# Entering a gated recurrence: one summed view of squares, and gate sums and weights put off

## The chip, the cores and the metric

The kernel runs on one core of a Trainium2 chip. The metric is the device time of one execution in microseconds. TensorE (PE in the profile, PEld for its weight loads) multiplies matrices into PSUM banks; VectorE (DVE), ScalarE (ACT) and GpSimd (POOL) work on elements; SyncE's queue (SPq) issues the DMAs of this kernel. Each engine takes its instructions in the order in which the finished program lists them, so an instruction that waits holds up everything behind it in its own queue.

## The reference

A trunk of two layers over 1024 tokens of width 1024. Each layer adds a token mixer and then a SwiGLU channel mixer to the residual; before each stands an RMS norm, modulated by shift and scale from a conditioning vector. Layer 0 mixes with a forgetting attention of 16 heads, layer 1 with gated linear attention (GLA) of 4 heads. What the change touches is the entry to layer 1's mixer, cut here to its core:

```python
h = modulate(rms_norm(x, norm1_g[i]), sh1, sc1)
q, k, v, r, a_lr = split(h @ w_in)
log_alpha = log_sigmoid(a_lr @ w_a2 + b_a) / GLA_TAU
b = cumsum(log_alpha, per chunk)          # the gate sums
q_in, k_in = q * exp(b), k * exp(-b)
o_intra = where(tril, q_in @ k_in.T, 0) @ v
k_dec = k * exp(b_last - b);  kv = k_dec.T @ v
S = exp(b_last) * S + kv;     o = o_intra + q_in @ S_prev
o = rms_norm(o) * g_o * silu(r)
```

Everything is float32. The kernel keeps that precision by splitting each matmul operand into a high part (rounded to the matmul's number format) and a low part (the rest) and adding three products: high by high, high by low, low by high.

## The kernel before, in words

Activations lie with the features on the partitions: eight tiles of 128 features by 1024 tokens, handled in two halves of 512 tokens. The mixer's normalized input is `h1`, eight pairs `h1[k].hi` and `.lo` (in the profile `h1h`, `h1l`).

**The entry.** The last block of layer 0's channel mixer finishes `x` tile by tile (L1156). `SumSq` squares each finished tile on ScalarE (L663) and adds squares in a tree (L670) on VectorE and GpSimd. For the second half it leaves four views unadded: the sum of squares 0 to 3, that of 4 and 5, square 6, and square 7. They are handed to `norm_mixer` (L1639), which for the second half keeps them in `half1`, and then issues `late_low`: two low parts of the first half's `h1` (L637) that were put off.

After that TensorE computes values and the gate's low-rank input for head 0: `gva(tp, ...)` makes 48 products of 272 columns for two token tiles, in three groups (high by high, high by low, low by high) of 2 x 8. `in_turn` lists 96 of them for `tp` 0 and 1, all of which need the first half of `h1` alone, and puts small matmuls of the second half's norm between them, one behind each product as the list `rms_later(..., each=13)` says: `sums(i, t)` (L597) sums view `i` of token tile `t` over the partitions with a vector of ones; `root` takes the mean (DVE, L606) and its power -1/2 (POOL, L607); after 13 more products `row(t)` (L613) spreads the result over the partitions; then `norm_half` makes the second half of `h1` from it on VectorE, ScalarE and GpSimd. Behind these 96 follow the keys of half 0, values of `tp` 2 (with the first gate product `gate_z` between), values of `tp` 3, queries of half 0, keys of half 1 (L2004, L1708).

**Gate sums.** `gate_z` (L1760) gives the gate's logits; `gate_sum` makes the logarithm of the sigmoid (ACT, L1770 and L1771; DVE, L1772) and its running sum per block of 128 tokens (DVE scan, L1775). For the next head this is done ahead by the generator `gate_ahead(h + 1)`: its first step does `gate_z`, its second `gate_sum` and a DMA that stores the result in `gsum_d` (L1785); `gate_back` (L1791) reads it back later. The two slots of the ring `kdr` serve both the sums made ahead (`b16a`, `t2a`) and the pair `kd` (`kdh`, `kdl`), the transposed decayed keys that `kd_trans` (L1820) makes, so `kdh` waits for the store.

**Queries and recurrence.** `head_front` multiplies query products by the gates' exponentials (L1863, tile `gy`, from the PSUM tile `gqp`) and splits them (L164, L165: `gq00`, `gq01`). `head_back` does the products within chunks (`at`, `ahl`, `go`) and the states (`kv`, `S_t`); `weave` alternates it with `r_proj`, the output gate's products (`gr`). Then the next head's values follow (`gv`).

**Weights.** `feed` is one list of weight loads in the order of use: for head 0 keys, queries and two output-gate weights, then for head 1 two value weights (`wv_0`, `wv_4`), keys and so on. A load is one DMA on SP, two casts on ScalarE (L207, high part) and four subtractions on GpSimd (L210, low part). `feed.fill()` loads until `feed.depth` weights lie ready.

**What sets the order.** The program is traced through a tile framework that simulates a timeline to put each engine's instructions in order before anything runs. `tc.issue_after(ins)` (and `tied`, which takes several) adds an order without a semaphore: what the block traces on the engine of `ins` stands behind `ins` in that engine's queue. `last_of("D")` is the instruction traced last on VectorE, "A" ScalarE, "P" TensorE, "G" GpSimd. Beside all this, `ada1` feeds in pieces of the next modulation (DMA L405, ACT L423, POOL L425).

Of the kernel before, what the change touches and what calls it, by code (L numbers as in the profile page):

```python
# [16 lines left out]
P = 128  # L17
S = 1024
D = 1024
# [35 lines left out]
def trunk(ctx, tc, x, c, ada_w, ada_b, norm1_g, norm2_g, ffn_w_in, ffn_w_out,  # L55
# [534 lines left out]
    def rms_later(ss, nm, psr, then, each=0):  # L590
# [26 lines left out]
                then(at["rb"])  # L617

        if each:
            one = [f for i in range(len(ss)) for t in range(4) for f in (None, lambda i=i, t=t: sums(i, t))]  # L620
            return one + [root] + [None] * each + [lambda t=t: row(t) for t in range(4)]
        return ([None] * 2 + [lambda t=t: sums(0, t) for t in range(4)] + [None] * 2
                + [lambda t=t: rest(t) for t in range(4)] + [root] + [None] * 6
# [1014 lines left out]

    def norm_mixer(hf, ss, tmp):  # L1639
        if hf:  # L1640
            half1.extend((ss, tmp))
            with tc.issue_after(last_of("D")):
                for low in late_low:
                    low()
            return
        hs1.extend(new_h("h1"))
        rb = rms_rows(ss, "100", Ring(psp, ["b3", "b4"]))
        gates = [(SPM, sp_ins[-1]), (RBM, last_ins())]
        norm_half(xs, hs1, 1, 0, rb, tmp)
        return gates  # L1650
# [53 lines left out]
    def gva(tp, w, ring, at):  # L1704

        ps = [ring([P, VA], F32, f"gva{tp}{i}") for i in range(2)]
        ks = [(w[k // 3], k % 3) for k in range(8)]
        mm = lambda i, a_, b_, s0=False, s1=False: lambda: nc.tensor.matmul(ps[i], a_, b_, start=s0, stop=s1)  # L1708
        hs = lambda part, k, i: getattr(h1[k], part)[:, psl(2 * tp + i)]
        products = []  # L1710
        for i in range(2):
            products += [mm(i, hs("hi", k, i), w_.hi[:, j, :], s0=k == 0) for k, (w_, j) in enumerate(ks)]
        for i in range(2):
            products += [mm(i, hs("hi", k, i), w_.lo[:, j, :]) for k, (w_, j) in enumerate(ks)]
        for i in range(2):
            products += [mm(i, hs("lo", k, i), w_.hi[:, j, :], s1=k == 7) for k, (w_, j) in enumerate(ks)]

        def evac():
            v = vr([P, 2, 2, 256], FR, f"gvt0{tp}")
            for i in range(2):  # L1720
                nc.vector.tensor_copy(at(2 * tp + i), ps[i][:, 256:VA])
            for i in range(2):
                split(v[:, 0, i], v[:, 1, i], ps[i][:, 0:256])
            return v
        return products, evac
# [112 lines left out]
    def head_front(h, b16, t2, ei, nmid, kin=None, wq=None, q0=None):  # L1838
# [14 lines left out]
        for hf in range(2):  # L1853
# [9 lines left out]
                nc.vector.scalar_tensor_tensor(y, ps, QS, f[:, cs], op0=ALU.mult, op1=ALU.mult)  # L1863
                split(t.hi[:, cs], t.lo[:, cs], y)
            if not h:
                next(ahead, None)
            elif not hf:
                kd = kd_tiles(h)
                kd_trans(h, kd, t2, 0)
        if not h:  # L1870
            kd = kd_tiles(h)
            kd_trans(h, kd, t2, 0)
        return kin, qt, kd
# [15 lines left out]
    def head_back(h, kin, qt, kd, t2, dec, vt, gs, need):  # L1889
# [44 lines left out]
        for g in range(2):  # L1934
            ahl = intra(g)
            yield 1.3
            if g == 0:
                kd_trans(h, kd, t2, 1)
                sp[1] = state(0)
                yield 0.79  # L1940
                if h < 3:
                    gnext.append(gate_back(h + 1))
# [66 lines left out]
    def second(rb):  # L2009
# [3 lines left out]

    p0, evac0 = gva(0, wv, pj, atok)
    p1, evac1 = gva(1, wv, pj, atok)
    in_turn(p0 + p1, rms_later(half1[0], "101", Ring(psp, ["b3", "b4"]),
                               second, 13))
    vt = [evac0(), evac1()]
    kin = key_tiles(0)
# [8 lines left out]
    in_turn(listed(k0, wk, 0), [None] * 10 + turns, last_of("P"))  # L2028
    ends()
    p2, evac2 = gva(2, wv, pj, atok)  # L2030
    in_turn(p2, [None] * 24 + [lambda: gate_z(0, (0,), bt)], last_of("P"))
    to0 = sm.tile([P, 4, NB], F32, tag="dec", name="dec0"), Tr([P, S], F32, "ei0")
    vt.append(evac2())
    gate_sum(0, bt, (0,))
# [1 line left out]
    key_evac(kin, k0, 0, *bt, to0[1], to0[0][:, 2])  # L2036
    ada1(5.1)
    p3, evac3 = gva(3, wv, pj, atok)
    in_turn(p3, [], last_of("P"))
    vt.append(evac3())  # L2040
    feed.depth = 1
    wq = feed.next()
# [6 lines left out]
    in_turn(listed(k1, wk, 1), [None] * 6 + [lambda: gate_z(0, (1,), bt)], last_of("P"))  # L2049
    k1_last = last_of("P")  # L2050
    gate_sum(0, bt, (1,))
    with tied(last_of("A")):
        feed.fill()
    b16, t2, ei, dec = gate_exps(0, bt, (1,), to0)
    key_evac(kin, k1, 1, b16, t2, ei, dec[1])
    for _ in range(3):
# [111 lines left out]
```

## Time and profile before

| what | value |
|---|---|
| runs | 2408.58, 2413.9, 2415.01 us; median 2413.9 |
| profiled execution | 2415.17 us, span 2413.3 us |
| mean granted TensorE clock | 0.994 |
| TensorE busy | 2370.4 us, 98% of the span |
| entrance of the recurrence | about 1312 to 1405 us of the span |
| HBM traffic | 269.25 MB read, 90.24 MB written |

A row of the timeline has the start in us from the span's start, the time in us, the engine, the line of the kernel, the operation, written tile and read tiles, the shape, and `xN` where N instructions are merged; in brackets stands how long the engine sat idle before it and what released it. A row of stretches has the limits, the length, the busy time and number of instructions of each engine, the granted clock (1.00 is full speed) and the share and rate of DMA.

### The profile page before, as it was taken

What the parts mean: (1) busy time and instruction counts of PE and PEld (TensorE: products, weight loads), DVE (VectorE), ACT (ScalarE), POOL (GpSimd) and SP (SyncE); (2) the same over time, 40 slices, a digit from 0 to 9 for tenths busy, and PEclk for the clock granted to TensorE, in tenths of its full rate; (3) what the DMA queues carried; (4) which work ended last, traced back from release to release, by engine and by line L of the source; (5) the groups of instructions that cost most, each with busy time, mean ns of one, the idle gap of its engine ahead of it and who ended that gap; (6) DMA issues with size and microseconds to landing.
All of it is one profiled execution on the core that took longest, in us unless ns stands there. A gap on an engine that the chain in (4) does not pass through costs nothing.

```text
span 2413.3 us, 36035 instructions
## 1 busy us (share of the span) xinstructions
PE 2370.4 (98%) x12318; PEld 2017.3 (84%) x12318; DVE 1675.1 (69%) x2794; ACT 1186.9 (49%) x2285; POOL 1206.7 (50%) x1074
## 2 busy tenths in 40 slices
PE   7999999999999999999999999999999999999998
PEld 6888888878888888888888888898888888888888
DVE  6577677676687877876687645446586767666787
ACT  4665556666544444445324756564344333345325
POOL 3343344433337878853364546573345656653362
PEclk9999999999999999999999999999999999999999
DMA  9233333123335555457665334445325434347664
GB/s 273 70 107 114 97 111 108 62 94 117 127 100 179 184 167 178 158 182 259 227 205 164 83 110 123 127 129 177 113 84 174 165 133 150 134 172 260 225 208 147
DMA packets 329407, 361.88 MB, mean 150 GB/s; under 512 B 24508, under 2 KB 253016, under 8 KB 329224
## 3 DMA queue, kind: packets, MB, share of 16 engines
q1 hardware_dynamic: 329032, 359.57, 46.2%
q8 instruction: 97, 1.59, 0.3%
q14 instruction: 86, 0.70, 0.1%
q10 hardware_dynamic: 192, 0.02, 0.0%
HBM read 269.25 MB, written 90.24 MB: 149 GB/s over the span
## 4 chain that ended last, share of the span: by engine, by line
PE 88%; ACT 3%; DVE 3%; DMA 2%; issue 1%; SPq 1%; POOL 1%; DVEq 0%; POOLq 0%; ACTq 0%
PE p_b L263 16%; PE p_b L262 16%; PE p_b L261 16%; PE o_b L1061 2%; PE t_b L1047 2%; PE qk_b L261 2%; PE qk_b L262 2%; PE qk_b L263 2%; PE s_b L1016 1%; PE s_b L1017 1%; PE gr_b L262 1%; PE gr_b L263 1%; PE vps_b L261 1%; PE gr_b L261 1%; PE vps_b L262 1%
## 5 line engine op out<-in xcount | busy, mean ns | idle before, releaser
L165 DVE TENSOR_TENSOR o_s<-xv_s,o_s 128x512 fp32r<-128x512 f32 (+1 forms) x376 | 338.0, 902 | 76.3 <-ACT o_s L164 75.7
L164 ACT CAST o_s<-xv_s 128x512 fp32r<-128x512 f32 (+1 forms) x376 | 218.0, 587 | 330.9 <-PE p_b L263 267.5
L1027 POOL TENSOR_SCALAR lp_s<-lp_s,st 128x128 f32<-128x128 f32 (+7 forms) x128 | 98.1, 771 | 266.3 <-DVE st L1026 223.4
L262 PE MATMUL p_b<-B,o_s 128*128 128x512 f32 x592 | 230.6, 390 | 0.0
L263 PE MATMUL p_b<-B,o_s 128*128 128x512 f32 x592 | 230.0, 389 | 0.0
L261 PE MATMUL p_b<-B,o_s 128*128 128x512 f32 x592 | 229.4, 389 | 0.0
L788 POOL TENSOR_TENSOR ex_s<-xv_s,xv_s 128x512 f32<-128x512 f32 (+1 forms) x64 | 85.1, 1329 | 255.0 <-DMA xv_s<-in_ffn_w_in_dram 92.9
L261 PE MATMUL p_b<-T,o_s 128*128 128x512 f32 x480 | 186.7, 389 | 0.0
L262 PE MATMUL p_b<-T,o_s 128*128 128x512 f32 x480 | 186.7, 389 | 0.0
L263 PE MATMUL p_b<-T,o_s 128*128 128x512 f32 x480 | 180.7, 389 | 0.0
L261 PEld LDWEIGHTS p_b<-B,o_s 128*128 128x128 f32 x592 | 111.1, 188 | 23.1
L262 PEld LDWEIGHTS p_b<-B,o_s 128*128 128x128 f32 x592 | 111.1, 188 | 23.0
L263 PEld LDWEIGHTS p_b<-B,o_s 128*128 128x128 f32 x592 | 111.1, 188 | 22.9
L1025 ACT ACTIVATE lp_s<-lp_s,st 128x128 f32<-128x128 f32 (+7 forms) x128 | 99.3, 776 | 62.7 <-DVE st L1021 60.2
L790 POOL TENSOR_TENSOR xv_s<-ex_s,xv_s 128x512 f32<-128x512 f32 (+1 forms) x64 | 89.1, 1393 | 58.2 <-DVE o_s L165 56.0
L164 ACT CAST pt_s<-t_b 128x512 fp32r<-128x512 f32 (+1 forms) x160 | 79.7, 547 | 73.7 <-PE t_b L1047 73.0
L1406 DVE TENSOR_TENSOR ex_s<-ex_s,p_b 128x512 f32<-128x512 f32 x140 | 94.2, 681 | 27.0 <-PE p_b L263 26.8
L425 POOL TENSOR_TENSOR ad_s<-ad_s,ad_s 128x512 f32<-128x512 f32 x62 | 90.1, 1453 | 41.6 <-ACT ad_s L423 31.4
L262 PEld LDWEIGHTS p_b<-T,o_s 128*128 128x128 f32 x480 | 90.1, 188 | 18.8
L261 PEld LDWEIGHTS p_b<-T,o_s 128*128 128x128 f32 x480 | 90.1, 188 | 18.8
L165 DVE TENSOR_TENSOR pt_s<-t_b,pt_s 128x512 fp32r<-128x512 f32 (+1 forms) x160 | 96.9, 632 | 12.7 <-ACT pt_s L164 12.4
L263 PEld LDWEIGHTS p_b<-T,o_s 128*128 128x128 f32 x480 | 90.1, 188 | 18.6
(1994 smaller groups left out, 7518.5 us busy)
## 6 DMA issues: line engine op xcount, KB each, us to landing
xv_s<-in_ffn_w_in_dram SPq DMA_DIRECT2D x176, 256.0 KB, 3.1
hid_B<-x SPq DMA_DIRECT2D x70, 512.0 KB, 2.7
ad_s<-in_ada_w_dram SPq DMA_DIRECT2D x384, 64.0 KB, 2.0
hid_T<-x SPq DMA_DIRECT2D x36, 512.0 KB, 2.8
xv_s<-in_ffn_w_out_dram SPq DMA_DIRECT2D x96, 192.0 KB, 4.5
ada_s<-in_ada_w_dram SPq DMA_DIRECT2D x128, 128.0 KB, 2.7
xv_s<-in_ffn_w_out_dram SPq DMA_DIRECT2D x40, 256.0 KB, 2.8
T2o<-hid_T SPq DMA_DIRECT2D x18, 512.0 KB, 9.8
```

The source lines that it names most:

```text
L164: nc.scalar.copy(hi, src)
L165: nc.vector.tensor_sub(lo, src, hi.bitcast(F32))
L261: nc.tensor.matmul(ps, ah, bh, start=start, stop=False)
L262: nc.tensor.matmul(ps, ah, bl, start=False, stop=False)
L263: nc.tensor.matmul(ps, al, bh, start=False, stop=stop)
L425: nc.gpsimd.tensor_add(acc, acc, raw)
L788: nc.gpsimd.tensor_add(s1, a21, a22)
L790: nc.gpsimd.tensor_sub(a11, s1, a11)
L1025: nc.scalar.activation(lp, lp, AF.Exp, bias=mcur, scale=-1.0, accum_out=st[:, qi, 2:3])
L1027: nc.gpsimd.tensor_scalar(lp, lp, st[:, qi, 3:4], 1.0, op0=ALU.mult, op1=ALU.mult)
L1047: nc.tensor.transpose(tp[:, i, :], lps[qi][:, psl(2 * b + jj)], ident)
L1406: nc.vector.tensor_add(d, d if src is None else dest(G, src), ps)
```

## The change

1. `norm_mixer`, second half: three additions on VectorE, each behind the one before, add the four views into the first (0 with 1, 2 with 3, then both); `half1` keeps that one view alone. `late_low` stands behind them.
2. `rms_later` with `each`: its list begins with 30 empty places, then come four `sums` over the one view (16 before, beginning behind the second product, every other place), then `root`, 13 empty places and the four rows.
3. `gva` returns its three groups apart, and the 96 products run as `p0[0] + p0[1] + p1[0] + p0[2] + p1[1] + p1[2]`; the later calls for `tp` 2 and 3 join the three groups, which gives the same order as before.
4. `head_front` of head 0: the second step of `gate_ahead` (gate sums of head 1 and their store) runs behind the loop over both halves, its VectorE instructions behind the last one traced there.
5. `feed`: at the fill after the second half's first gate sum two weights lie ready instead of three; the depth is then 1, and in `head_back` of head 0, behind the second `kd_trans`, it is 3 again and a fill follows, its ScalarE instructions behind the last one traced. The two value weights of head 1 are loaded there.

```diff
         if each:
-            one = [f for i in range(len(ss)) for t in range(4) for f in (None, lambda i=i, t=t: sums(i, t))]
+            one = [None] * 30 + [lambda t=t: sums(0, t) for t in range(4)]
             return one + [root] + [None] * each + [lambda t=t: row(t) for t in range(4)]
...
         if hf:
-            half1.extend((ss, tmp))
+            half1.extend((ss[:1], tmp))
+            for a, b_ in ((0, 1), (2, 3), (0, 2)):
+                with tc.issue_after(last_of("D")):
+                    nc.vector.tensor_add(ss[a], ss[a], ss[b_])
             with tc.issue_after(last_of("D")):
                 for low in late_low:
                     low()
...
-        products = []
+        products = [[], [], []]
         for i in range(2):
-            products += [mm(i, hs("hi", k, i), w_.hi[:, j, :], s0=k == 0) for k, (w_, j) in enumerate(ks)]
-        for i in range(2):
-            products += [mm(i, hs("hi", k, i), w_.lo[:, j, :]) for k, (w_, j) in enumerate(ks)]
-        for i in range(2):
-            products += [mm(i, hs("lo", k, i), w_.hi[:, j, :], s1=k == 7) for k, (w_, j) in enumerate(ks)]
+            products[0] += [mm(i, hs("hi", k, i), w_.hi[:, j, :], s0=k == 0) for k, (w_, j) in enumerate(ks)]
+            products[1] += [mm(i, hs("hi", k, i), w_.lo[:, j, :]) for k, (w_, j) in enumerate(ks)]
+            products[2] += [mm(i, hs("lo", k, i), w_.hi[:, j, :], s1=k == 7) for k, (w_, j) in enumerate(ks)]
...
             if not h:
-                next(ahead, None)
+                if not hf:
+                    next(ahead, None)
             elif not hf:
                 kd = kd_tiles(h)
                 kd_trans(h, kd, t2, 0)
         if not h:
+            with tied(last_of("D")):
+                next(ahead, None)
             kd = kd_tiles(h)
             kd_trans(h, kd, t2, 0)
...
                 kd_trans(h, kd, t2, 1)
+                if not h:
+                    feed.depth = 3
+                    with tied(last_of("A")):
+                        feed.fill()
                 sp[1] = state(0)
...
-    in_turn(p0 + p1, rms_later(half1[0], "101", Ring(psp, ["b3", "b4"]),
+    in_turn(p0[0] + p0[1] + p1[0] + p0[2] + p1[1] + p1[2], rms_later(half1[0], "101", Ring(psp, ["b3", "b4"]),
                                second, 13))
...
-    in_turn(p2, [None] * 24 + [lambda: gate_z(0, (0,), bt)], last_of("P"))
+    in_turn(sum(p2, []), [None] * 24 + [lambda: gate_z(0, (0,), bt)], last_of("P"))
...
     gate_sum(0, bt, (1,))
+    feed.depth = 2
     with tied(last_of("A")):
         feed.fill()
+    feed.depth = 1
     b16, t2, ei, dec = gate_exps(0, bt, (1,), to0)
```

2 lines of the change are left out of this document (1 added, 1 removed).

## The prediction

> **What bounds the kernel now.** I read the page first, then TensorE's waits, then busy time and granted clock by stretch.
>
> ```profile
> PE 2370.4 (98%) x12318; PEld 2017.3 (84%) x12318; DVE 1675.1 (69%) x2794; ACT 1186.9 (49%) x2285; POOL 1206.7 (50%) x1074
> ```
>
> TensorE is busy 98% of the span, so a change pays only where TensorE waits, does work that can go, or runs at a lower clock. Of its waits, two (waiter, releaser, us in total, times, longest) lie in the recurrence's entrance, where the change is; a third, of 0.76 us, is among the sums quoted below:
>
> ```profile
> PE go_b L261 <- DVE gy_s L1863: 3.2, 1, 3.2
> PE go_b L263 <- DVE ahl_s L165: 1.0, 1, 1.0
> ```
>
> Stretches (us, length, then busy us and instructions of PE, PEld, DVE, ACT, POOL; granted clock; DMA):
>
> ```profile
> 1311.97:1334.18 22.21, 21.45 (x138) 21.22 (x136) 10.44 (x19) 9.11 (x17) 9.35 (x10) 0.77 0.40 131
> 1313.86:1317.27 3.41, 2.65 (x22) 2.43 (x21) 3.11 (x4) 1.66 (x4) 2.37 (x3) 1.00 0.54 214
> 1317.27:1327.51 10.24, 10.24 (x48) 10.24 (x47) 0.77 (x3) 0.45 (x2) 3.78 (x5) 0.50 0.35 98
> 1378.71:1382.12 3.41, 2.81 (x16) 2.04 (x14) 3.17 (x1) 3.38 (x5) 3.24 (x4) 1.00 0.37 88
> 1385.54:1388.95 3.41, 1.17 (x9) 0.91 (x8) 3.41 (x3) 0.28 (x2) 1.48 (x1) 1.00 0.44 112
> 1388.95:1395.78 6.83, 5.88 (x15) 4.77 (x16) 2.24 (x4) 2.45 (x4) 2.57 (x2) 0.50 0.29 89
> ```
>
> Two half-clock spells, of 10.24 and 6.83 us (three and two times 3.41), follow stretches of 3.41 us in which the array had little to stream: the 0.76 us wait with one-column sums around it, and the 3.19 us wait. They cost 5.1 and 3.4 us. The stretch at 1378.71, busy 2.81 us, was followed by no drop.
>
> **First part: the entrance (1311.97 to 1334.18).** It now holds 96 value products, 16 sums over `ones` (four views, four token tiles; two matmuls each) and 4 row broadcasts.
>
> ```profile
> 1313.31 0.49 PE L1708 MATMUL gva_b<-wva6h_s,h1h 128*128 128x272 f32 x2
> 1313.65 0.28 PE L597 MATMUL sp_b<-ones,se_s 128*128 128x1 f32 x2
> 1313.78 0.50 PE L1708 MATMUL gva_b<-wva0h_s,h1h 128*128 128x272 f32 x2
> 1315.04 0.38 PE L597 MATMUL sp_b<-ones,se_s 128*128 128x1 f32 x2 [0.76 <-DVE se_s L670]
> ```
> ```profile
> 1328.21 0.38 PE L613 MATMUL rb_b<-ident,rs 128*128 128x128 f32 x2
> 1328.35 0.37 PE L1708 MATMUL gva_b<-wva0h_s,h1h 128*128 128x272 f32 x1
> 1328.56 0.53 PE L1708 MATMUL gva_b<-wva3h_s,h1h 128*128 128x272 f32 x3
> 1328.93 0.41 PE L1708 MATMUL gva_b<-wva6h_s,h1h 128*128 128x272 f32 x2
> ```
>
> Three products take 0.37 us (1328.56 to 1328.93), so one 0.125. Two products and a sum take 0.47 (1313.31 to 1313.78), so a sum 0.22. Row and product take 0.35 (1328.21 to 1328.56), so a row 0.22. Check: 96 x 0.125 + 16 x 0.22 + 4 x 0.22 + 0.76 + 5.1 = 22.3, against 22.21 measured.
>
> After: twelve sums go (-2.6), three VectorE additions come, and the first sum stands behind product 31, at 1311.97 + 31 x 0.125 = 1315.85. Are the additions done by then?
>
> ```profile
> L670 DVE TENSOR_TENSOR se_s<-se_s,se_s x7: 680/691/1780, 1285.0 to 2378.7; 128x512 f32<-128x512 f32 x7
> ```
> ```profile
> 1315.68 0.63 ACT L663 ACTIVATE se_s<-x 128x512 f32<-128x512 f32 x1 [1.75 <-DVE x L1156]
> ```
> ```profile
> 1315.57 1.40 DVE L637 SCALAR_TENSOR_TENSOR h1l<-te_s,modc,h1h 128x512 fp32r<-128x512 f32 x2
> ```
> ```profile
> 1323.73 1.02 POOL L607 TENSOR_TENSOR rs<-rs,mhalf 128x4 f32<-128x4 f32 x1 [7.50 <-DVE rs L606]
> ```
>
> No. The last square ends at 1316.31. The first addition runs ahead of it; the second and third follow, 0.69 each by the median of that row (up to 1.78 beside POOL), so the view is whole at 1317.7. The wait of 0.76 becomes one of 1.85 (up to 4.0 with both additions slow). The two late lower halves (1.40 for both) move behind the additions and end at 1319.1; only `p0[2]`, product 49 on, reads them, and TensorE is there at 1317.7 + 4 x 0.35 + 15 x 0.125 = 1321.0. The power (1.02) starts about 1319.3, ends by 1320.5 and is covered by the same products; without cover it would cost 1.4. So the stretch is 12.0 + 0.9 + 0.9 + 1.85 = 15.65: **6.6 us less**, if the clock holds.
>
> Clock: the new wait lies in two stretches of the 3.41 grid. From 1313.86 products stream some 2.0 us (58%), from 1317.27 some 2.1 us (62%). The dropped stretch had 11 products, 1.4 us (40%; the other L597 and waits); the kept one was busy 2.81 (82%). That is midway, and the grid need not lie the same in every run. Ends: 0 and two stretches at half clock, 3.4. I take half of one drop, **0.9**. The Trainium skill, "TensorE: Matmul & The Clock Gate", in Part 1 and its closing table, says that the clock falls after an idle window of about 3.4 us and warns of gaps over about 3 us. By that the price here is 0; the drop after a gap of only 0.76 us disagrees, so I do not rely on it.
>
> What is late next: the second half's normalization starts with the last row, here 1328.56, then about 1322.4 (-6.1), while TensorE comes 6.6 earlier; and the first pair's evacuations (two of 0.43 and two small copies, about 1.2 us of VectorE) now follow the normalization instead of preceding it.
>
> ```profile
> 1326.12 0.43 DVE L165 TENSOR_TENSOR gvt_s<-gva_b,gvt_s 128x256 fp32r<-128x256 f32 x1 [0.44 <-ACT gvt_s L164]
> ```
> ```profile
> 1341.75 0.68 DVE L1738 TENSOR_TENSOR aT<-aps_b,aT 16x512 fp32r<-16x512 f32 x1
> ```
> ```profile
> 1343.30 0.40 PE L1760 MATMUL z_b<-aT,w2t 128*128 128x512 f32 x1
> ```
>
> `aT` ended 0.87 before the gate product; 0.5 + 1.2 - 0.87 leaves a wait of **0.8** (0 if the queue puts `aT` first, 1.7 if slower). Entrance: -6.6 + 0.9 + 0.8 = **-4.9**.
>
> **Second part: gate sums and value weights.** VectorE's queue before the 3.19 us wait:
>
> ```profile
> 1378.95 3.55 DVE L165 TENSOR_TENSOR ahl_s<-atz_s,ahl_s 128x512 fp32r<-128x512 f32 x1 [1.56 <-ACT ahl_s L164]
> 1382.42 0.68 DVE L165 TENSOR_TENSOR gq00l_s<-gy_s,gq00h_s 128x512 fp32r<-128x512 f32 x1
> 1383.02 1.21 DVE L1772 TENSOR_TENSOR t2a_s<-b16a_s,t2a_s 128x1024 f32<-128x1024 f32 x1
> 1384.16 1.78 DVE L165 TENSOR_TENSOR gq01l_s<-gy_s,gq01h_s 128x512 fp32r<-128x512 f32 x1
> 1385.86 3.41 DVE L1775 TENSOR_TENSOR_SCAN b16a_s<-rm,t2a_s 128x512 f32<-128x512 bf16 x2
> 1389.19 0.66 DVE L1863 SCALAR_TENSOR_TENSOR gy_s<-gqp_b,b_s 128x512 f32<-128x512 f32 x1
> ```
> ```profile
> 1376.74 1.13 ACT L207 CAST wv_4h_s<-wv_s 128x512 fp32r<-128x512 f32 x2
> ```
> ```profile
> 1377.89 2.81 POOL L210 TENSOR_TENSOR wv_4l_s<-wv_s,wv_4h_s 128x256 fp32r<-128x256 f32 x4
> ```
>
> The next head's subtraction (1.21) and scans (3.41) stand before `gy`, which empties the bank that `go_b` needs; the edit puts them behind the last query split. The value weights go from ScalarE (1.13 for each of two) and POOL (2.81 each), so `ahl` no longer lies beside `wv_4l`. `gy` then ends, even with `ahl` at 3.55, at 1382.5 + 0.68 + 0.69 + 0.66 = 1384.5. TensorE reached that wait at 1386.7, and 1.0 earlier without the first one. Both waits and the second spell go: **-1.0 - 3.2 - 3.4 = -7.6**.
>
> Moved with them: the store and reading back of the gate sums, and two weight loads on SP. Queued behind them:
>
> ```profile
> 1394.38 0.37 SPq L1785 DMA_DIRECT2D gsum_d<-b16a_s  x1
> ```
> ```profile
> 1389.88 0.62 ACT L164 CAST gq01h_s<-gy_s 128x512 fp32r<-128x512 f32 x1 [4.06 <-DVE gy_s L1863]
> ```
> ```profile
> 1397.26 0.59 ACT L164 CAST kdh_s<-kdt_b 128x512 fp32r<-128x512 f32 x1 [4.86 <-DMA gsum_d<-b16a_s]
> ```
> ```profile
> 1404.90 0.59 ACT L164 CAST kdh_s<-kdt_b 128x512 fp32r<-128x512 f32 x1 [4.26 <-PE kdt_b L1820]
> ```
> ```profile
> 1404.26 0.60 PE L1820 MATMUL kdt_b<-ident,t_s 128*128 128x128 f32 x4
> ```
> ```profile
> 1405.29 0.27 PE L261 MATMUL gv_b<-wv_0h_s,h1h 128*128 128x256 f32 x1
> ```
>
> `kdh` takes over the slot of the gate sums and waits for their store; the second transposes follow, then the second `kdh`. The weights' casts are now tied behind that cast on ScalarE, and `gv` needs them when the output-gate products end, 1405.29 now, 1397.7 after (entrance left out). After `gy` come a cast (0.62), a split (0.69), the subtraction and the scans: they end at 1390.5 (1389.27 now), or 1387.7 where `ahl` takes 0.7. The tie orders VectorE's entries alone; the exponential and logarithm on ScalarE may stay, and wherever they go they find the 4.06 us for which it now idles. The store, which stood in SP's queue until 1394.38, issues between 1388 and 1394.4 and takes 2.9; casts and transposes bring the second `kdh` to 1393.3 at best, 1400 at worst. First half-cast 0.57 and first POOL piece 0.70 later `gv` can start: 1394.6 to 1401.3. TensorE waits 0 to 3.6; with the transposes at their present place (1396.7 on this count) about 1.5, and a little for POOL's pace. I take **2.0**; the upper end is 3.6 and one half-clock stretch, 5.3. A gain is excluded: before, `gv` waited for nothing.
>
> The Trainium skill, "SBUF — State Buffer", Who interferes with whom and the lock rule above it, has VectorE operations with two SBUF inputs and POOL's reads shut each other out for a whole instruction. The 3.55 us `ahl`, which ended just after POOL's pieces, agrees. By it the moved POOL pieces would hold up the state steps' subtractions instead, two by 0.7 us: 1.4, if value products did not cover them.
>
> **Sum.** -4.9 - 7.6 + 2.0 = -10.5. The sum is made against the profiled execution:
>
> ```profile
> span 2413.3 us, 36035 instructions
> ```
>
> With 1.9 around the span it took 2415.17 us: **2404.7**, 9.2 or 0.38% below the median 2413.9 of the runs; the profiled execution lies 1.3 above that median.
>
> **Rivals.**
> - The weights' wait decides: 5.3 in place of 2.0, **2408.0**. For it: casts tied behind a cast that itself hangs on a store in SP's queue. Against: with the long wait gone, ScalarE and the modulation work that fills SP run on.
> - The entrance loses the clock: 3.4 in place of 0.9, and 1 us more in the additions: **2408.2**. For it: 58% is nearer to 40 than to 82.
> - The second part does nothing, because the order planned for VectorE puts other work before `gy`: only -4.9, **2410.3**. Against: every named piece is tied.
> - Slower: the store of the gate sums falls behind one more group of modulation loads.
>
> ```profile
> SPq L405 <- POOL ad_s L425: 75.9, 38, 11.2
> ```
>
> The longest such wait was 11.2 us. Store at 1405.6, `gv` at 1412.5: TensorE is idle 13.7 and then loses 3.4 of clock, 17.1 against the 12.5 of gains: **2419.8**. It decides once the second `kdh` ends after 1405.5, where it ends now; so it needs the whole chain to stay in place while TensorE moves up.
>
> **How the numbers follow.** Forecast 0.48 (2402 to 2407.5), weights 0.17, clock 0.12, no second part 0.07, slower 0.16. About 0.3%, 7.2 us, is what a measurement of this kernel tells from no change; that line lies at 2406.7. Faster: 0.44 of the forecast and 0.08 of the next two, 0.52. Slower by 7.2 or more: 0.09, the bad half of the last rival; the rest is the same, 0.39. Range 2400 (no wait for weights, clock kept, chain shorter) to 2415 (into the last rival; 0.15 lies above).
>
> **What would show it.** `sp_b` falls from 32 matmuls to 8, with one wait near 1.85; clock 1.00 from 1317 to 1327; stretch near 16 us; no wait on `gy` at `go_b`; `kdh` still waiting for the store, and a wait of about 2 at the first `gv`. I am wrong if the first `gv` or `kv` waits over 5 us, or if half-clock spells return in both places.

## The result and the profile after

| | before | after |
|---|---|---|
| runs | 6, 2408.58 to 2416.01 us | 6, 2398.71 to 2404.26 us |
| median | 2414.37 us | 2401.2 us |
| profiled execution | 2415.17 us | 2401.05 us |
| mean granted clock | 0.994 | 0.996 |

The ratio of the times is 0.9949 [0.9937, 0.9962]: 0.5% faster. Two profiled executions show 14.1 us less, the medians 13.2.

The first lines of the page after:

```profile
span 2399.3 us, 36002 instructions
...
PE 2358.5 (98%) x12294; PEld 2006.9 (84%) x12294; DVE 1674.9 (70%) x2797; ACT 1185.9 (49%) x2285; POOL 1203.4 (50%) x1074
```

Where did the 14 us come from? A ledger of when TensorE reaches the same work in both traces tells it. First the rows of before that the prediction does not show (timeline, TensorE; the first key product of head 1 and the first value product of head 2), then those of after: first value product of the entrance, first key product behind them, first gate product, then first value product of head 1, first key product of head 1, first value product of head 2. Lines of `kernel.py` have moved by up to eight (`gva` L1708 is L1711 now).

```profile
1436.05 0.40 PE L261 MATMUL gk_b<-h1h,w_h_s 128*128 128x512 f32 x1
...
1496.01 0.28 PE L261 MATMUL gv_b<-wv_0h_s,h1h 128*128 128x256 f32 x1
```
```profile
1312.44 0.54 PE L1711 MATMUL gva_b<-wva0h_s,h1h 128*128 128x272 f32 x3
...
1329.66 0.39 PE L2012 MATMUL gk_b<-h1h,w_h_s 128*128 128x512 f32 x1
...
1340.09 0.40 PE L1761 MATMUL z_b<-aT,w2t 128*128 128x512 f32 x1
...
1395.81 0.40 PE L261 MATMUL gv_b<-wv_0h_s,h1h 128*128 128x256 f32 x2
...
1426.23 0.39 PE L261 MATMUL gk_b<-h1h,w_h_s 128*128 128x512 f32 x1
...
1481.95 0.28 PE L261 MATMUL gv_b<-wv_0h_s,h1h 128*128 128x256 f32 x1
```

| TensorE begins | before | after | difference | gained since the row above |
|---|---|---|---|---|
| entrance, values | 1311.97 | 1312.44 | +0.47 | |
| first keys | 1334.18 | 1329.66 | -4.52 | 5.0 |
| first gate product | 1343.30 | 1340.09 | -3.21 | -1.3 |
| values of head 1 | 1405.29 | 1395.81 | -9.48 | 6.3 |
| keys of head 1 | 1436.05 | 1426.23 | -9.82 | 0.3 |
| values of head 2 | 1496.01 | 1481.95 | -14.06 | 4.2 |

From there to the end the two traces keep their distance (the spans differ by 14.0). So the gain comes in three pieces: 3.7 in the entrance, 6.3 in head 0's recurrence, and 4.2 in head 1's recurrence, on which the prediction has no term. Between the last two lie another 0.3, and 0.5 is lost ahead of the entrance, which begins later.

**The entrance after.** Waits of TensorE between 1305 and 1470, and the stretches of the clock there:

```profile
PE sp_b L597 <- DVE se_s L1644: 1.6, 1, 1.6
PE gva_b L1711 <- DVE gvt_s L165: 1.1, 1, 1.1
PE go_b L261 <- ACT mib L1967: 0.4, 1, 0.4
```
```profile
1312.44:1329.66 17.22, 15.59 (x114) 15.40 (x112) 11.01 (x18) 7.85 (x15) 9.06 (x10) 0.90 0.52 168
1316.89:1320.30 3.41, 2.20 (x18) 2.23 (x19) 2.52 (x5) 0.64 (x2) 0.52 (x1) 1.00 0.76 239
1320.30:1323.71 3.41, 3.41 (x18) 3.41 (x17) 0.00 (x0) 0.00 (x0) 3.26 (x5) 0.50 0.43 118
```

The half-clock spell of 10.24 us is now one stretch of 3.41, and it again follows a stretch in which the array was not busy throughout: 2.20 us of 3.41, one-column sums included. The sums stand where the prediction put them, and the wait ahead of them is there:

```profile
1315.76 2.19 DVE L1644 TENSOR_TENSOR se_s<-se_s,se_s 128x512 f32<-128x512 f32 x3
```
```profile
1318.10 0.35 PE L597 MATMUL sp_b<-ones,se_s 128*128 128x1 f32 x2 [1.63 <-DVE se_s L1644]
...
1337.89 0.62 PE L1711 MATMUL gva_b<-wva0h_s,h1h 128*128 128x272 f32 x3 [1.10 <-DVE gvt_s L165]
```

The second row is new. The third pair of values waits 1.10 us for its bank, because the evacuation of the first pair now stands behind the normalization on VectorE (it begins at 1337.33; before, at 1326.12, it came ahead of it).

**The recurrence after.** Of the waits of 3.2 and 1.0 us at `go_b` nothing is left but 0.4 for another releaser. VectorE, then SP, ScalarE, GpSimd:

```profile
1374.92 0.68 DVE L165 TENSOR_TENSOR ahl_s<-atz_s,ahl_s 128x512 fp32r<-128x512 f32 x1
1375.52 0.68 DVE L1864 SCALAR_TENSOR_TENSOR gy_s<-gqp_b,b_s 128x512 f32<-128x512 f32 x1
...
1381.41 3.39 DVE L1776 TENSOR_TENSOR_SCAN b16a_s<-rm,t2a_s 128x512 f32<-128x512 bf16 x2
```
```profile
1385.55 0.37 SPq L1786 DMA_DIRECT2D gsum_d<-b16a_s  x1
```
```profile
1388.38 0.59 ACT L164 CAST kdh_s<-kdt_b 128x512 fp32r<-128x512 f32 x1 [4.04 <-DMA gsum_d<-b16a_s]
...
1390.52 0.58 ACT L164 CAST kdh_s<-kdt_b 128x512 fp32r<-128x512 f32 x1
1390.99 1.14 ACT L207 CAST wv_0h_s<-wv_s 128x512 fp32r<-128x512 f32 x2
```
```profile
1392.47 2.83 POOL L210 TENSOR_TENSOR wv_0l_s<-wv_s,wv_0h_s 128x256 fp32r<-128x256 f32 x4
```

`gy` comes at 1375.52 (1389.19 before), ahead of the scans; `ahl` takes 0.68 us (3.55 before). Before, GpSimd was busy beside `ahl` with the four pieces of `wv_4l` and, right behind them, a piece of the modulation; after, it idles until `ahl` is nearly done (first before, then after):

```profile
1380.66 1.29 POOL L425 TENSOR_TENSOR ad_s<-ad_s 128x512 f32<-128x512 f32 x1
```
```profile
1375.42 1.33 POOL L425 TENSOR_TENSOR ad_s<-ad_s,ad_s 128x512 f32<-128x512 f32 x1 [1.58 <-ACT ad_s L423]
```

`kdh` does wait for the store, as forecast, but the store issues 8.8 us earlier than before (1385.55 against 1394.38; 3.2 of that is the entrance), so the second `kdh` and the casts of `wv_0` are done by 1392.1, and the first GpSimd piece (0.70 of the four in 2.83) by 1393.2. The first value product at 1395.81 has no wait in its row.

**Head 1's recurrence.** Two rows of TensorE's waits before and the stretches around them, which the prediction passed over:

```profile
PE kv_b L261 <- ACT kdh_s L164: 0.9, 1, 0.9
...
PE kdt_b L1820 <- DVE kdl_s L165: 0.5, 1, 0.5
```
```profile
1460.63:1464.04 3.41, 2.28 (x18) 2.14 (x19) 1.82 (x4) 2.15 (x4) 3.33 (x3) 1.00 0.75 199
1464.04:1467.46 3.42, 3.42 (x11) 2.65 (x10) 2.89 (x4) 1.17 (x3) 3.34 (x4) 0.50 0.50 130
```

After has neither the two waits nor the spell: 0.9 + 0.5 + 1.7 = 3.1 of the 4.2. A wait of 0.5 on `mib` at 1477.68 is gone as well; 0.6 stays unexplained. What made `kdh` late can be read from ScalarE, before and after:

```profile
1450.13 0.72 ACT L423 ACTIVATE ad_s<-ad_s,cblk 128x512 f32<-128x512 f32 x1 [1.54 <-DMA ad_s<-in_ada_w_dram]
1450.87 1.28 ACT L1771 ACT_TABLE_LOAD   x1
1452.16 1.06 ACT L1771 ACTIVATE t2a_s<-t2a_s 128x1024 f32<-128x1024 f32 x1
```
```profile
1437.91 1.28 ACT L1772 ACT_TABLE_LOAD   x1
1439.20 1.06 ACT L1772 ACTIVATE t2a_s<-t2a_s 128x1024 f32<-128x1024 f32 x1
...
1441.45 0.72 ACT L423 ACTIVATE ad_s<-ad_s,cblk 128x512 f32<-128x512 f32 x1 [0.15 <-DMA ad_s<-in_ada_w_dram]
```

Before, a piece of the next modulation (L423) stood between the exponential and the logarithm of head 2's gates and waited 1.54 us for its DMA; everything behind it (logarithm, scans, store, `kdh`) came later. After, the planned order has that piece behind the logarithm. Head 1's `kdh` needs the slot that the store frees, as in head 0.

### The profile page after: what moved, and what is told of

The parts are those of the page before. It is cut to its first block, busy times and chain, and to the rows that moved or that the text cites. A ratio compares the mean times of both kernels' runs of the same rounds, so it can differ in the third digit from the quotient of the medians.

```text
span 2399.3 us, 36002 instructions
## 1 busy us (share of the span) xinstructions
PE 2358.5 (98%) x12294; PEld 2006.9 (84%) x12294; DVE 1674.9 (70%) x2797; ACT 1185.9 (49%) x2285; POOL 1203.4 (50%) x1074
## 4 chain that ended last, share of the span: by engine, by line
PE 89%; DVE 3%; DMA 2%; ACT 2%; issue 1%; POOL 1%; SPq 1%; DVEq 0%; POOLq 0%; ACTq 0%
PE p_b L263 16%; PE p_b L262 16%; PE p_b L261 16%; PE o_b L1061 2%; PE t_b L1047 2%; PE qk_b L261 2%; PE qk_b L263 2%; PE qk_b L262 2%; PE s_b L1016 1%; PE gr_b L262 1%; PE gr_b L261 1%; PE vps_b L261 1%; PE vps_b L262 1%; PE gr_b L263 1%; PE vps_b L263 1%
## 5 line engine op out<-in xcount | busy, mean ns | idle before, releaser
L165 DVE TENSOR_TENSOR pt_s<-t_b,pt_s 128x512 fp32r<-128x512 f32 (+1 forms) x160 | 96.9, 632 | 13.2 <-ACT pt_s L164 12.9
```

The source lines that it names most:

```text
L165: nc.vector.tensor_sub(lo, src, hi.bitcast(F32))
```

## The experiments

Three questions. First, which part brings the gain: the sums (parts 1 to 3 of the change), the gate sums (part 4) or the weights (part 5)? Second, what is the entrance worth, where the clock decides? Third, can the wait that the sums still have be covered? Ratios are to the kernel before, measured beside it on the same chip.

### The sums alone

Parts 1 to 3 of the change, nothing of 4 and 5 (of the lines against before, those of part 3 are cut):

```diff
-            one = [f for i in range(len(ss)) for t in range(4) for f in (None, lambda i=i, t=t: sums(i, t))]
+            one = [None] * 30 + [lambda t=t: sums(0, t) for t in range(4)]
...
-            half1.extend((ss, tmp))
+            half1.extend((ss[:1], tmp))
+            for a, b_ in ((0, 1), (2, 3), (0, 2)):
+                with tc.issue_after(last_of("D")):
+                    nc.vector.tensor_add(ss[a], ss[a], ss[b_])
```

> The sums' part alone (three additions, one view, the new order of products); gate sums and value weights as before. Theory: the changed kernel's trace against the one before shows the values' stretch 5.0 us shorter, a start 0.5 later and a new wait of 1.1 at the third pair of values, so about -3.7, to 2410.7 against 2414.4; the waits of 3.2 and 1.0 us at go_b and a half-clock spell behind them are there as before. Rival (the sums' part also moves the work that follows, so that the later waits shrink by themselves): 2407 or less, with less than 2 us of wait at go_b.

Measured: 2409.84 us, 0.9997 [0.9986, 1.0008] (12 runs). In its profile the entrance looks like that of the changed kernel, and the recurrence like that of before (stretch, then waits between 1305 and 1470):

```profile
1312.80:1330.30 17.50, 15.78 (x114) 15.38 (x113) 11.11 (x19) 8.17 (x15) 9.37 (x10) 0.90 0.51 166
```
```profile
PE go_b L261 <- DVE gy_s L1864: 3.2, 1, 3.2
PE go_b L263 <- DVE ahl_s L165: 2.4, 2, 1.3
PE sp_b L597 <- DVE se_s L1644: 1.7, 1, 1.7
PE gva_b L1711 <- DVE gvt_s L165: 1.1, 1, 1.1
```

Of the 2.4 on `ahl`, 1.0 lies in head 0's recurrence and 1.3 in head 1's (1468.04). So the stretch is 4.7 us shorter than in the profile of before, and the kernel is no faster: the interval reaches from 3.4 us of gain to 1.9 of loss.

### Gate sums and weights alone

Parts 4 and 5, with the 16 sums as before:

```diff
             if not h:
-                next(ahead, None)
+                if not hf:
+                    next(ahead, None)
...
+            with tied(last_of("D")):
+                next(ahead, None)
...
+                if not h:
+                    feed.depth = 3
+                    with tied(last_of("A")):
+                        feed.fill()
...
+    feed.depth = 2
     with tied(last_of("A")):
         feed.fill()
+    feed.depth = 1
```

> Gate sums and value weights put off, the sums as before (16 over four views). Theory: both waits at go_b and the half-clock spell at 1389 go, 6.3 us up to the next head's values, and another 4.1 in head 1, where the wait for kdh and its half-clock stretch go: -10.4, to 2404.0; the entrance keeps its wait of 0.76 and a half-clock spell of about 10 us in most runs. Rival (head 1's gain comes from the shift of the whole plan, not from this part): head 1 keeps its wait of 0.9 for kdh, and the time is 2408.

Measured: 2402.15 us, 0.9963 [0.9948, 0.9978] (8 runs, four at 2398.51 to 2400.13 and four at 2404.18 to 2407.94): most of the gain. The profile, of an execution of 2398.51 us, brought something that no theory had. The entrance is the code of before, its sums wait 0.9 us, and no spell follows:

```profile
1310.30:1327.90 17.60, 16.73 (x138) 16.51 (x136) 10.52 (x19) 9.22 (x17) 9.45 (x11) 1.00 0.50 165
```

The same code that took 22.21 us in the profile of before takes 17.60 here. Head 1's `kdh` has no wait.

### Sums and gate sums, weights early

The whole change without part 5; the two value weights load where they did before:

```diff
                 kd_trans(h, kd, t2, 1)
-                if not h:
-                    feed.depth = 3
-                    with tied(last_of("A")):
-                        feed.fill()
...
-    feed.depth = 2
     with tied(last_of("A")):
         feed.fill()
-    feed.depth = 1
```

> The changed kernel with the value weights loaded early, as before. Theory: the scans behind the last query split are what frees the bank for go_b: the 3.2 us wait and the spell go, while the 1.0 us wait at ahl (beside the weights' pieces on POOL) stays: about 2402.5, 1 to 1.5 above the changed kernel. Rival (the weights' casts on ScalarE and pieces on POOL held the chain): go_b still waits 2 us or more on gy, 2405 to 2408.

Measured: 2405.73 us, 0.9974 [0.9963, 0.9985] (11 runs). VectorE, then waits between 1305 and 1470:

```profile
1375.48 3.55 DVE L165 TENSOR_TENSOR ahl_s<-atz_s,ahl_s 128x512 fp32r<-128x512 f32 x1 [1.55 <-ACT ahl_s L164]
...
1380.27 0.69 DVE L1864 SCALAR_TENSOR_TENSOR gy_s<-gqp_b,b_s 128x512 f32<-128x512 f32 x1
```
```profile
PE go_b L263 <- DVE ahl_s L165: 2.3, 2, 1.3
...
PE kv_b L261 <- ACT kdh_s L164: 0.9, 1, 0.9
PE kdt_b L1821 <- DVE kdl_s L165: 0.6, 1, 0.6
```

The wait on `gy` is gone, so part 4 does what it says. `ahl` still takes 3.55 and costs 1.0 in head 0's recurrence (the other 1.3 lies in head 1's, at 1463.80), and head 1 keeps its `kdh` waits. These the theory left out, so its 2402.5 missed by 3.2; the rival's time fits, its wait of 2 us on `gy` does not. This is better than the sums alone (0.9997), just clear of it by the intervals too, but short of the whole change (0.9949, and 0.9963 below).

### Sums and weights, gate sums early

The whole change without part 4:

```diff
             if not h:
-                if not hf:
-                    next(ahead, None)
+                next(ahead, None)
...
-            with tied(last_of("D")):
-                next(ahead, None)
```

> The changed kernel with the next head's gate sums where they were. Theory: gy stays behind 4.6 us of subtraction and scans, but ahl and ScalarE are 2 to 3 us earlier without the weights, so go_b waits 0 to 1.5 us for gy in place of 3.2 and the clock holds: 2402 to 2404. Rival (only the gate sums matter): a wait of 3 us and a half-clock spell at go_b, 2407 to 2408.

Measured: 2400.08 us, 0.9955 [0.9940, 0.9970] (5 runs), not told apart from the whole change. Between 1305 and 1470 its waits are 1.7 at the sums, 1.1 at the third value pair and 0.4 on `mib`, the same three as after: no `gy`, no `ahl`, no `kdh`. So with the weights put off, part 4 adds nothing that can be seen.

### The weights alone

The kernel before with part 5 only:

```diff
                 kd_trans(h, kd, t2, 1)
+                if not h:
+                    feed.depth = 3
+                    with tied(last_of("A")):
+                        feed.fill()
...
+    feed.depth = 2
     with tied(last_of("A")):
         feed.fill()
+    feed.depth = 1
```

> The kernel before with the value weights of the next head put off, and nothing else of the change. Theory: the weights decide both gains outside the sums: no wait above 0.5 us for gy or ahl at go_b, no half-clock spell behind them, and head 1 plans the modulation pieces behind the logarithm, so no wait for kdh there: 2402, as with both put off. Rival (the gate sums are needed as well while the sums of squares are as before): 2 to 3 us of wait for gy stay, 2406 or more.

Measured: 2405.45 us, 0.9962 [0.9947, 0.9977] (6 runs), not told apart from parts 4 and 5 together (0.9963). Although no line of it touches the gate sums, the wait on `gy` is gone. VectorE shows why:

```profile
1381.06 0.68 DVE L1863 SCALAR_TENSOR_TENSOR gy_s<-gqp_b,b_s 128x512 f32<-128x512 f32 x1
...
1383.26 1.23 DVE L1772 TENSOR_TENSOR t2a_s<-b16a_s,t2a_s 128x1024 f32<-128x1024 f32 x1 [1.52 <-ACT t2a_s L1771]
```

`gy` now stands ahead of the subtraction without being told to. That the timeline which orders the program now has `gy` ready earlier, with two weight casts and two sets of GpSimd pieces out of the way, is likely but not shown. Its profile, of 2406.28 us, drew the long end of the entrance:

```profile
1312.84:1336.50 23.66, 23.00 (x137) 22.78 (x136) 10.45 (x18) 9.04 (x17) 9.25 (x10) 0.71 0.38 123
```

Its six runs lie at 2399.14 and 2399.99 (mean clock 0.998 and 0.999) and at 2405.12 to 2407.34 (0.994 and 0.995). A spell like that one, of 13.65 us and so 6.8 us of loss, is about the distance between these groups. That the upper four runs all had it is argued from the clock; only one of them was profiled. So the theory's waits were right, and its 2402 lies between the two groups.

The ledger of the result, made for each of these profiles, sets the parts side by side (us gained on before; head 0 from the first gate product to the values of head 1, head 1 from its keys to the values of head 2):

| parts in the kernel | head 0's recurrence | head 1's recurrence |
|---|---|---|
| sums | 1.1 | 1.2 |
| sums, gate sums | 5.8 | 0.05 |
| weights | 6.4 | 2.8 |
| sums, weights | 6.5 | 4.1 |
| gate sums, weights | 6.3 | 3.4 |
| all | 6.3 | 4.2 |

A second profile of each of the last two, further down, gives 6.3 and 2.9, and 6.2 and 3.9. Either of parts 4 and 5 brings head 0's gain (the sums alone only have one stretch at half clock there in place of two). Only with the weights put off does head 1's recurrence gain more than 1.2.

### The sums behind 46 products

The whole change, with the first sum 15 products later, past the end of the additions:

```diff
-            one = [None] * 30 + [lambda t=t: sums(0, t) for t in range(4)]
+            one = [None] * 45 + [lambda t=t: sums(0, t) for t in range(4)]
```

> The changed kernel with the four sums behind 46 products in place of 31 (45 empty places). Theory: product 46 ends about when the three additions do, so the wait of 1.6 us is under 0.3 and the half-clock stretch at the entrance goes in every run: the stretch of the values falls from 17.2 to about 14; the wait at the third pair of values, which hangs on VectorE, grows from 1.1 to 2 or 2.5; in all -2, to 2399, with less scatter. Rival (VectorE's normalization sets this stage's end, not TensorE): the wait there takes all of it, 4 us or more, and the time stays at 2401.

Measured: 2397.23 us, 0.9937 [0.9924, 0.9951] (6 runs, five of them within 2396.1 to 2397.6, the sixth 2403.57).

```profile
1310.80:1324.60 13.80, 13.80 (x113) 13.79 (x112) 10.28 (x18) 6.75 (x14) 7.81 (x10) 1.00 0.61 198
```
```profile
PE z_b L1761 <- DVE aT L1739: 1.1, 1, 1.1
```

No wait, no spell, TensorE busy 13.80 of 13.80 us: 3.4 less than after. The wait at the third value pair did not grow, as the theory had it, but went: VectorE here evacuates the first pair ahead of the normalization (1319.53). In its place stands one of 1.1 on `aT`, which VectorE still makes behind the normalization (1334.26).

### A free bank for the low-rank input, and that without part 4

As in the last run, and the transposed low-rank input in another PSUM bank; then the same without part 4 (both against the whole change, the 45 empty places of the last run cut):

```diff
-    turns, ends = a_turn(0, atok, pj)
+    turns, ends = a_turn(0, atok, Ring(psp, ["b4"]))
```

> As the one with sums behind 46, and the transposes of the gate's input write to the bank that the row broadcast has left, so that the third pair of values finds two empty banks. Theory: the wait of 1 to 2.5 us for the first pair's evacuation goes; what ends next is the gate's input for the first gate product, 0 to 1.5 us of wait: 2397.5. Rival (the normalization's h1 halves arrive as late as the bank): a wait for h1 of 2 us at the same place, 2399.

Measured: 2399.6 us, 0.9945 [0.9932, 0.9959]. The wait for the bank, which the theory wanted to remove, had gone with the last run already. The wait on `aT` stays at 1.1 as VectorE's queue is as late as there, so the other bank gains nothing.

```diff
-    turns, ends = a_turn(0, atok, pj)
+    turns, ends = a_turn(0, atok, Ring(psp, ["b4"]))
...
             if not h:
-                if not hf:
-                    next(ahead, None)
+                next(ahead, None)
...
-            with tied(last_of("D")):
-                next(ahead, None)
```

> As the last, with the next head's gate sums where they were before. Theory: with the weights put off the gate sums' place makes no difference beyond 1 us: 2397 to 2398.5, no wait for gy at go_b. Rival: with TensorE 3 us earlier the scans are on the path again, a wait for gy of 1 us or more, 2400.

Measured: 2397.41 us, 0.9935 [0.9923, 0.9948]; no wait on `gy`. A second pair, beside sums and weights against the whole change, in which part 4 makes no difference that can be told.

### The change and its second half once more, on one chip

The whole change again, and parts 4 and 5 again, this time measured side by side. The second differs from the first by parts 1 to 3, of which one line is shown:

```diff
-            one = [None] * 30 + [lambda t=t: sums(0, t) for t in range(4)]
+            one = [f for i in range(len(ss)) for t in range(4) for f in (None, lambda i=i, t=t: sums(i, t))]
```

> The changed kernel once more, beside the one without the sums' part, on one chip. Theory: its entrance holds one wait of 1.6 us and at most one half-clock stretch: 2399 to 2404, median 2401.5.

> Gate sums and value weights put off, the sums as before, once more. Theory: without a half-clock spell at the entrance (values' stretch 17.6) it is as fast as the changed kernel or faster, with one (22 to 24) it is 5 to 7 us slower, so two groups of runs, near 2399 and near 2405.5, and a median that is 0 to 4 above the changed kernel's. Rival (the sums' part is worth its 6.6 us in every run): one group, near 2406.

Measured: the whole change 2403.38 us, 0.9963 [0.9950, 0.9976] (7 runs); without the sums 2405.57, 0.9968 [0.9956, 0.9980] (11 runs). The medians differ by 2.2 us, the ratios by 0.0005, well inside both intervals. The two groups that the theory expected cannot be told apart: the eleven runs spread from 2401.01 to 2409.23. The rival, 6.6 us in every run, fails too: the profiled execution had the old sums and took 17.60 for the stretch. The stretch in the two profiles, first the whole change, then without the sums:

```profile
1311.40:1328.80 17.40, 15.67 (x113) 15.41 (x113) 10.97 (x19) 8.03 (x15) 9.30 (x10) 0.90 0.52 167
```
```profile
1313.10:1330.70 17.60, 16.77 (x138) 16.55 (x137) 10.51 (x19) 9.21 (x17) 9.41 (x10) 1.00 0.52 165
```

### The gate product later

The sums behind 46, and the first gate product behind 37 value products instead of 25, to cover the wait on `aT`:

```diff
-    in_turn(sum(p2, []), [None] * 24 + [lambda: gate_z(0, (0,), bt)], last_of("P"))
+    in_turn(sum(p2, []), [None] * 36 + [lambda: gate_z(0, (0,), bt)], last_of("P"))
```

> Sums behind 46 products, and the first gate product behind 37 products of the third pair instead of 25. Theory: the wait of 1.1 us for aT goes, and the gates, 1.5 us later, still come in time: 2396, 1 below the one with sums behind 46. Rival (the gates' chain is on the path): the microseconds come back as waits at the first chunk products or at go_b, 2397 to 2399.

Measured: 2398.08 us, 0.9943 [0.9930, 0.9957]. The wait on `aT` falls from 1.1 to 0.2, and a wait of 0.5 on the low-rank input (1348.79) and one of 0.9 on `mib` at `go_b` (0.4 and 0.5 in the two profiles of the whole change) stand in its place. The time fits the rival's 2397 to 2399. The 1.4 on `ahl` lies in head 1's recurrence, where the weights alone have 0.9 of it too:

```profile
PE go_b L261 <- ACT mib L1967: 0.9, 1, 0.9
PE go_b L261 <- ACT ahl_s L164: 0.8, 1, 0.8
PE go_b L263 <- DVE ahl_s L165: 0.6, 1, 0.6
```

No gain over the sums behind 46. Measured beside the whole change on the same chip, whose seven runs lie at 2400.15 to 2404.47, its runs lie at 2397.2 to 2400.42.

**The better version** is therefore the sums behind 46 products: 0.9937 of the time before, and 0.9945, 0.9935 (the other bank, with and without part 4) and 0.9943 (later gate product) with it in place, against 0.9949 and 0.9963 for the change in its two measurements. Only the last of these was measured beside the change; the others lean on the ratios, whose intervals overlap with that of the change's first measurement.

## Why the prediction was right, and where it was not

The sign was right, and so was the second part's mechanism; the time forecast, 2404.7, lies 3.5 us above the median, which is also just below the 2402 to 2407.5 of its main case. Of its signs three came: eight matmuls on `sp_b` behind one wait of 1.63, no wait on `gy`, `kdh` waiting for the store. Three did not: the clock fell between 1317 and 1327, the stretch took 17.2 and not some 16, and the first `gv` waited for nothing. The forecast was 10.5 below the profiled execution; the profiles differ by 14.1. By its own steps:

| step | forecast | measured on the profiles |
|---|---|---|
| entrance to the first gate product | -4.9 | -3.7 |
| wait at the sums | 1.85 | 1.63 |
| a dropped clock there | 0.9 | 1.7, one stretch |
| late evacuations | 0.8, at `aT` | 1.10, at the third value pair |
| waits and spell of head 0's recurrence | -7.6 | -6.3 |
| wait for the value weights | +2.0 | 0 |
| head 1's recurrence | no term | -4.2 |

**The entrance.** The prices of the single instructions held. 12.0 for the products, 0.9 each for sums and rows, the measured 1.63 of wait and 1.7 for a stretch of 3.41 at half clock make 17.1; the stretch took 17.22. The step that failed is the price of what was removed: the prediction counted the 5.1 us of lost clock in the profile of before as something that every run pays. It does not hold. Four profiles with the old sums took 22.21, 17.60, 23.66 and 17.60 us; five with the new ones took 17.22, 17.50, 18.72, 17.27 and 17.40 (the 18.72, of sums and gate sums, with a spell of two stretches). Set against an old entrance at full clock the new one is worth nothing, since the twelve sums that go (2.6) come back as a longer wait and as a dropped stretch; set against one with a spell it is worth 5 to 6. From the first gate product on 1.1 is then given back to the bank. The runs average over all this, and there the sums are worth nothing that can be told: 0.9997 alone, 0.9963 against 0.9968 on top of the rest. A gain of 1 or 2 us on the mean is not excluded, and the runs scatter less: with the weights and gate sums put off they spread over 9.4 and 8.2 us with the old sums, over 5.6 and 4.3 with the new ones.

**The clock in the new entrance.** The prediction took half of one drop, for a wait split over two stretches, with 58% and 62% of streaming; its rival "the entrance loses the clock" held that 58% is nearer to 40 than to 82. One whole drop came in after and in three more of the five profiles of this entrance (mean clock 0.90 over the entrance), two in the fifth (0.82), but not at 58%. In every trace the clock changes only at edges that lie a whole number of 3.4133 us apart, and against the work these edges lie differently in each profile. In after they are at 1316.89 and 1320.30, so the wait fell into one stretch. Counted as the prediction counts, by products alone (0.125 us each, an estimate of 0.23 for one of 512 columns by their distance in the rows), that stretch streamed 36%. The nine profiles, counted so:

| entrance | stretch with the wait ahead of the sums | next stretch |
|---|---|---|
| old sums: before; weights | 37%; 40% | half clock |
| old sums: gate sums and weights, again | 43% | full clock |
| old sums: gate sums and weights | 51%, then 47% | full clock |
| new sums: sums and weights; sums; all again; all; sums and gate sums | 19, 23, 28, 36, 41% | half clock |

In the third row the wait crosses an edge at 1313.24 (the spell that ends at 302.89 in this trace gives the grid, 296 steps earlier). So the same code kept the clock or lost it with the place of the wait on the grid. And 59 to 61%, in the stretch around the wait of 1.1 that follows the entrance, kept the clock in three profiles (sums and weights; all again; the sums behind 46 without part 4), so the rival's reason does not hold; its drop came because the wait was not split. That the line lies between 41 and 43% is an estimate from these nine; no run shifted the wait on purpose. The Trainium skill, "TensorE: Matmul & The Clock Gate", Part 1 and closing table, would have the clock fall after an idle window of about 3.4 us; a drop behind a wait of 1.63 does not agree. The same Part 1 of the Trainium skill says that the activity window is free-running and that the same kernel's slow phase varies from run to run; with that the 17.60 to 23.66 us for one code and the moving edges agree.

**The recurrence.** The order named was the one that decided: `gy` behind subtraction and scans. Both waits and the spell went. 7.6 was too much by about 0.5, because the spell of 6.83 held only 5.88 us of TensorE's work, so that it cost 2.9 and not 3.4; a new wait of 0.4 on `mib` is the next piece, and 0.4 stays unexplained. Which part did it was beyond the prediction, which gave the gate sums the leading role: either part alone removes the wait on `gy`; the weights' part also removes that of 1.0 on `ahl`, and it alone removes head 1's on `kdh`. (Waits of 0.2 to 0.8 on `ahl` that some profiles show with the weights put off lie in head 1's recurrence, at 1455 to 1467.) `ahl` at 3.55 with the weights early and 0.68 with them late is the plainest pair: beside the first GpSimd worked without a pause until 1381.95, on the four pieces of `wv_4l` and the modulation piece behind them, and `ahl` ended 0.55 later; the second ran while GpSimd idled, but for its last 0.2. The Trainium skill, "SBUF — State Buffer", on who interferes with whom, has a VectorE operation with two inputs in SBUF and a GpSimd operation that reads SBUF shut each other out, and both rows agree.

**The weights' wait.** The chain was as described. The forecast's times leave the entrance out, and TensorE comes to the recurrence 3.2 us earlier after than before (the row of the first gate product), so 3.2 has to be added to the times after. On that count the scans ended at 1388.0 (forecast 1387.7 where `ahl` takes 0.7, else 1390.5), the store went at 1388.8 (1388 to 1394.4), the second transposes began at 1393.0 (taken at 1396.7), the second `kdh` ended at 1394.3 (1393.3 to 1400), the weights were ready at 1396.4 (1394.6 to 1401.3), and TensorE came for them at 1399.0 (1397.7). Every link lies within its bounds, close to the early end, and the wait is 0, the lower end of 0 to 3.6. The term that was mis-sized is the 2.0. It took `ahl` at 3.55 for safety, though the same paragraph says that its neighbour on GpSimd goes, and the transposes at their present place, while these moved up behind the earlier `kdh`.

**Head 1.** The prediction's list of waits stopped at head 0's recurrence; the waits of 0.9 and 0.5 and the spell at 1464 stood in the same view. Even with them in sight their end would not have followed from the diff: it came from another place of one modulation piece in the planned order. Both other profiles with the weights early kept these waits or part of them, in step with how long L423 waited between exponential and logarithm: 0.6 on `kdl` alone with the sums, where L423 waited 0.34, and 0.9 and 0.6 with sums and gate sums, where it waited 1.66. All profiles with the weights put off have no such piece between the two, and no wait on `kdh` in head 1. That it is the weights is shown; why the planned order then has L423 behind the logarithm was not tried.

**The rivals.** The slower case needed the store behind one more group of modulation loads; the store moved forward instead, by 5.6 us against TensorE. (Its 13.7 us of idle time do not follow from its own 1412.5 and 1397.7, which give 14.8.) "The second part does nothing" fell with the same rows. So it is partly luck that the total lies in the range. On the profiles 1.2 too much in the entrance and 1.3 too much in the recurrence stand against 2.0 of wait that did not come and 4.2 in head 1 that nobody forecast. On the runs the entrance's 4.9 cannot be told from nothing, and head 1 fills its place.

## What to carry to other kernels

A half-clock spell in one profile is no sure gain: look at the times and mean clocks of several runs before its loss is put into a sum. A reduction that feeds TensorE belongs behind enough independent products that it is finished when its turn comes; here 15 products more took wait and spell out of the profiled entrance (13.80 us against 17.22), while 12 sums fewer cannot be seen in the times. A load that can be moved off a crowded stage may be worth more than any reordering inside it, and a plan made anew may give or take some microseconds a stage later, so the waits of the next stages belong in the list from the start.

## What the runs showed of the hardware

- A kernel's spread goes with the clock: 25 runs of the kernel before, on one chip, lie between 2405.33 us at a mean clock of 0.998 and 2418.78 at 0.991. The profiled run with 2415.17 had 0.994. That spread, 0.56%, is as large as the whole effect of the change.
- Half-clock spells came in whole stretches of 3.41 us: 3.41, 6.83, 10.24 and 13.65. One followed a wait of only 0.76 us with sums of a single column around it, another a wait of 1.63; two profiles of the old sums had a wait of 0.9 and 0.8 at the same place and no spell. What a stretch of the 3.41 us grid streams, sums not counted, parts the nine entrances: 19 to 41% ahead of a half-clock stretch, 43 to 51% without one (an estimate; no run shifted the wait on purpose).
- Between exponential and logarithm ScalarE loaded a table for 1.28 us, and a foreign piece between the two delayed the logarithm by what it waited for, 1.54 us of DMA, beside its own 0.72.
